# Depthwise convolution: one group's taps moved to TensorE between the key and value products

## The chip, the cores and the metric

The kernel runs on one core of a Trainium2 chip. The metric is the device time of one execution in microseconds (us). TensorE is PE in the profile's rows (PEld its weight loads), VectorE is DVE, ScalarE is ACT, GpSimd is POOL, and SyncE (SP) issues the loads.

## What is computed

Two blocks of two layers each over 512 positions of width 1024, in float32. The change lies in the second block's second layer, in its convolution module. The part of the reference that matters:

```
def conv_module(xn, w_in, b_in, dw_w, dw_b, ln_g, ln_b, w_out):
    h = xn @ w_in + b_in
    a, gate = jnp.split(h, 2, axis=-1)
    h = a * jax.nn.sigmoid(gate)
    h = lax.conv_general_dilated(
        h, dw_w[:, None, :], window_strides=(1,), padding=[(CONV_WIDTH - 1, 0)],
        dimension_numbers=('NWC', 'WIO', 'NWC'), feature_group_count=D_CONV) + dw_b
    h = jax.nn.silu(layernorm(h, ln_g, ln_b))
    return h @ w_out
...
    k = rmsnorm((memn @ wk).reshape(bsz, m_len, C_HEADS, C_HEAD_DIM), k_gain)
    v = (memn @ wv).reshape(bsz, m_len, C_HEADS, C_HEAD_DIM)
```

The convolution has 31 taps for each of 1024 channels. The keys and values are those of the cross attention that follows. They depend on the memory input alone, so they can be made while the convolution runs.

## The kernel before

**Layout.** Channels lie on the partitions in the module: eight groups g = 0 to 7 of 128 channels by 512 positions. A weight tile is loaded by SP into `raw` (three buffers) and split into two halves for a product in three passes: ACT writes the high half (L228), and DVE or GpSimd subtracts for the low half (L229, `W.low` names the engine). There are eight buffers `hl`, so a split must wait until TensorE is done with the tile eight places earlier.

**Input products.** `prod(g, j, ...)` makes the two products of a group in two PSUM banks. Then `evac(g, ...)` applies the gate: ACT reads both banks (L1439, L1440), and DVE writes `hp[:, g]` (L1441), with 30 columns of padding. No tap of a group can start before its gate.

**Taps.** A tap multiplies a shifted view of `hp` with one weight per channel. There are three ways:

- DVE: `dve_tap` (L1509, L1511) sums in a PSUM bank named by `where`.
- GpSimd: `pool_tap` sums in SBUF, in `y`. The first tap is one operation on GpSimd (L1499). For each further one ACT makes the product `m` (L1502; four buffers, so ACT's product waits for GpSimd's addition of the one four places earlier), and GpSimd adds it (L1503).
- TensorE: `diagonals` has ACT write the weights of a tap as a diagonal matrix `dg` (L1537), and `by_diagonals` multiplies it with `hp` into a bank (L1544).

`join(g)` adds DVE's or TensorE's bank to `y` (L1514, on DVE). Groups 0 to 5 had 20 taps on DVE and 11 on GpSimd. Groups 6 and 7 had 14 on TensorE, 11 on DVE and 6 on GpSimd.

**Order.** The program's order on each engine is written by a planner with a clock of its own. `steps` are TensorE's steps in order. `feed(us)` ahead of a step puts as many taps on DVE's and GpSimd's queues as fit by the costs in `T_TAP` (DVE, GpSimd). Delayed work is queued with `X.at`. Each engine then runs its instructions in that order, and waits where an operand is late.

**Keys and values.** `memory_kv` gives 16 steps of twelve matmuls: four each for two halves of the keys, then for two halves of the values. Before them the memory input is transposed on TensorE (L337, four times four blocks) and split into `xh` and `xl` (L325, L326). After each half of the keys the result is normed (ACT L999, GpSimd L321 and L322, DVE L1006), transposed (L1011) and copied (ACT L1012). Values are copied (ACT L1023).

**Layer norm.** Its statistics run over all channels. `means` sums the groups of `y` with a matrix of ones on TensorE (L1559), 16 matmuls for two halves of the positions, into banks 4 and 5. Then `norm_half(0)` and later `norm_half(1)` do for each group: subtract the mean (`spread`: DVE L1588, ACT's square L1589, temporaries `s` with three buffers), sum the squares (`total`: TensorE L1596), then once reduce (DVE L1599), take the root (GpSimd) and transpose (`across`, L1606), and scale (`scale`: DVE L1610, ACT L1611 and L1612; `apply`: DVE L1616). The output product runs on position blocks of 128; its first two need half 0. The sums of half 1 stand between its matmuls.

Before, 13 of the 16 steps of keys and values stood ahead of the layer norm, and the last three were put between the operations of `norm_half(0)` (`fill`), with GpSimd doing low halves.

## Time and profile before

| | |
|---|---|
| time, median of 3 runs | 2859.72 us (2858.93 to 2860.82) |
| the profiled execution's own time | 2861.09 us |
| its span, first to last instruction | 2859.3 us |
| TensorE, busy and mean clock granted | 96% of the span, 0.984 |
| VectorE, ScalarE, GpSimd, busy | 45%, 35%, 17% |
| window of the taps' operations on GpSimd | 2100.5 to 2235.8 us |
| window of DVE's taps and joins | 2102.2 to 2276.7 us |
| window of the layer norm's first half | 2278.0 to 2308.2 us |

All times in the document count from the span's start. A busy TensorE is not one at its peak, since the ends of matmuls are modelled. A clock of 1.0 is 2.4 GHz, and 0.5 is 1.2 GHz. The shares are means over a program whose stages have different limits.

### The profile page before, as it was taken

To read this page: it belongs to the slowest core of one execution; us is meant where nothing else is said; L and a number is where in the kernel's file an instruction comes from. 1 tells how busy PE (TensorE), PEld (TensorE's weight loads), DVE (VectorE), ACT (ScalarE), POOL (GpSimd) and SP (SyncE) were. 2 spreads that over 40 slices of the span, in tenths; PEclk is the share of its full clock that TensorE was granted. 3 is DMA by queue.
4 is the path that set the end of the run, shared out by engine and by line. 5 is a ranking of instruction groups with operands and counts; after the bars stand their busy time and mean duration, and the time that the engine had idled before them with its cause. 6 is when DMAs were issued, how large, how long until landed. Compare 5 with 4: busy or idle time off the path is not lost.

```text
span 2859.3 us, 34280 instructions
## 1 busy us (share of the span) xinstructions
PE 2744.4 (96%) x13688; PEld 2302.1 (81%) x13688; DVE 1294.8 (45%) x1952; ACT 1012.5 (35%) x1774; POOL 472.9 (17%) x483
## 2 busy tenths in 40 slices
PE   7999999999899999999999999999998789999999
PEld 7888888889788888888677888888886568888887
DVE  4565222444464323344974443223389744422232
ACT  3434222333434222334454532223266244322231
POOL 3231000013131000022450310000059223100000
PEclk9999999999999999999999999999999889999999
DMA  4222322323222333322132212333232112133231
GB/s 148 79 72 74 113 93 96 111 62 108 68 74 81 98 101 103 108 75 86 52 129 74 99 50 100 107 98 110 89 123 81 66 46 95 47 101 103 89 118 52
DMA packets 76191, 255.95 MB, mean 90 GB/s; under 512 B 10368, under 2 KB 11776, under 8 KB 76032
## 3 DMA queue, kind: packets, MB, share of 16 engines
q1 hardware_dynamic: 76032, 253.77, 27.0%
q8 instruction: 107, 1.75, 0.2%
q14 instruction: 52, 0.43, 0.0%
HBM read 251.64 MB, written 2.10 MB: 89 GB/s over the span
## 4 chain that ended last, share of the span: by engine, by line
PE 83%; DVE 7%; POOL 4%; ACT 4%; issue 2%; DMA 0%; POOLq 0%; ACTq 0%; DVEq 0%; SPq 0%
PE b L315 26%; PE b L317 25%; PE b L316 25%; POOL y L1503 2%; DVE b L1511 1%; PE b L337 1%; PE b L1395 1%; ACT hl L228 1%; DVE hl L229 1%; DVE mask L1173 1%; POOL sm L322 1%; PE b L712 1%; DVE mask L1178 0%; PE b L733 0%; PE b L747 0%
## 5 line engine op out<-in xcount | busy, mean ns | idle before, releaser
L315 PE MATMUL b<-xh,hl 128*128 128x512 f32 (+1 forms) x1728 | 641.9, 371 | 1.6 <-ACT xh L325 1.6
L316 PE MATMUL b<-xl,hl 128*128 128x512 f32 (+1 forms) x1728 | 640.8, 371 | 1.7 <-DVE xl L326 1.7
L317 PE MATMUL b<-xh,hl 128*128 128x512 f32 (+1 forms) x1728 | 640.2, 370 | 0.0
L229 DVE TENSOR_TENSOR hl<-raw,hl 128x1024 fp32r<-128x1024 f32 (+1 forms) x411 | 489.5, 1215 | 157.6 <-ACT hl L228 154.5
L228 ACT CAST hl<-raw 128x1024 fp32r<-128x1024 f32 (+1 forms) x468 | 464.5, 1016 | 102.3 <-PE b L317 65.5
L315 PE MATMUL b<-hl,xh 128*128 128x512 f32 (+2 forms) x1152 | 442.4, 384 | 3.4 <-ACT xh L1612 1.7
L317 PE MATMUL b<-hl,xl 128*128 128x512 f32 (+2 forms) x1152 | 425.8, 370 | 4.5 <-DVE xl L326 4.3
L316 PE MATMUL b<-hl,xh 128*128 128x512 f32 (+2 forms) x1152 | 425.6, 369 | 1.8 <-DVE hl L229 1.8
L315 PEld LDWEIGHTS b<-xh,hl 128*128 128x128 f32 x1728 | 326.8, 189 | 58.6 <-ACT xh L325 2.8
L316 PEld LDWEIGHTS b<-xl,hl 128*128 128x128 f32 x1728 | 326.9, 189 | 57.6 <-DVE xl L326 2.7
L317 PEld LDWEIGHTS b<-xh,hl 128*128 128x128 f32 x1728 | 326.6, 189 | 55.4
L506 DVE TENSOR_TENSOR hraw<-sg,b 128x512 f32<-128x512 f32 (+1 forms) x96 | 61.8, 643 | 675.2 <-PE b L317 658.4
L505 ACT ACTIVATE sg<-b 128x512 f32<-128x512 f32 (+1 forms) x96 | 54.0, 563 | 674.8 <-PE b L317 674.7
L315 PE MATMUL b<-hl,hh 128*128 128x512 f32 x704 | 274.5, 390 | 0.0
L317 PE MATMUL b<-hl,hlw 128*128 128x512 f32 x704 | 274.0, 389 | 0.0
L316 PE MATMUL b<-hl,hh 128*128 128x512 f32 x704 | 274.0, 389 | 0.0
L315 PEld LDWEIGHTS b<-hl,xh 128*128 128x128 f32 x1152 | 221.4, 192 | 34.0 <-issue 8.3
L317 PEld LDWEIGHTS b<-hl,xl 128*128 128x128 f32 x1152 | 220.6, 191 | 31.4 <-DVE xl L326 5.7
L316 PEld LDWEIGHTS b<-hl,xh 128*128 128x128 f32 x1152 | 221.6, 192 | 25.6 <-DVE hl L229 3.1
L326 DVE TENSOR_TENSOR hlw<-hraw,hh 128x512 fp32r<-128x512 f32 x88 | 60.5, 691 | 210.5 <-ACT hh L325 210.5
L317 PEld LDWEIGHTS b<-hl,hlw 128*128 128x128 f32 x704 | 132.2, 188 | 27.5
L316 PEld LDWEIGHTS b<-hl,hh 128*128 128x128 f32 x704 | 132.2, 188 | 27.3
(272 smaller groups left out, 2968.2 us busy)
## 6 DMA issues: line engine op xcount, KB each, us to landing
raw<-in_ws SPq DMA_DIRECT2D x400, 512.0 KB, 3.5
raw<-in_ws SPq DMA_DIRECT2D x64, 384.0 KB, 3.1
x<-in_x SPq DMA_DIRECT2D x4, 512.0 KB, 6.3
mem<-in_mem SPq DMA_DIRECT2D x4, 512.0 KB, 5.7
out<-x SPq DMA_DIRECT2D x4, 512.0 KB, 2.6
raw<-in_ws SPq DMA_DIRECT2D x4, 336.0 KB, 2.9
gain<-in_g_mix_pre SPq DMA_DIRECT2D x2, 512.0 KB, 5.5
gain<-in_g_mix_post SPq DMA_DIRECT2D x2, 512.0 KB, 5.1
```

The lines of the kernel that those rows point to most:

```text
L228: self.nc.scalar.copy(t[:, 0, :w], r[:, :w])
L229: self.low.tensor_sub(t[:, 1, :w], r[:, :w], t[:, 0, :w].bitcast(F32))
L315: PE.matmul(o, lh, rh, start=first, stop=False)
L316: PE.matmul(o, lh, rl, start=False, stop=False)
L317: PE.matmul(o, ll, rh, start=False, stop=last)
L322: G.tensor_tensor(dst, dst, nhalf[:, :n], op=OP.pow)
L326: (low or V).tensor_sub(dl, src, dh.bitcast(F32))
L337: PE.transpose(b[:, kk * P:(kk + 1) * P], xn[:, k * P:(k + 1) * P], ident)
L505: S.activation(sg[:, c0:c1], gb[:, c0:c1], AF.Silu)
L506: V.tensor_mul(hraw[:, n, c0:c1], sg[:, c0:c1], ub[:, c0:c1])
L712: PE.matmul(s[hh][:, :n], qkT["aq"][rs, pr, cols(t)], qkT["ak"][rs, pr, :n], start=True, stop=True)
L1503: G.tensor_add(y[:, g, :], y[:, g, :], m)
```

## The change

Group 6 is no longer shared with TensorE: groups 0 to 6 have 19 taps on DVE and 12 on GpSimd, and group 7 has 28 on TensorE, 3 on GpSimd and none on DVE. The 28 diagonals are made four at a time, four such tiles ahead, and TensorE multiplies them in seven pieces of four, between the transposes of the memory input and after every second step of keys and values. Group 6 now sums in bank 4, group 7 in bank 7. The planner's cost of a tap is lower on both engines. All 16 steps of keys and values stand ahead of the layer norm; from the ninth on GpSimd does the low halves, and in the layer norm DVE does again. The two transposes after the first go to banks 0 and 1.

```
-NPOOL = (11,) * 6 + (6, 6)
-NPE = 14
-KV_LN = 13
-AT_PE = 12
-T_TAP = (0.78, 1.35)
+NPOOL = (12,) * 7 + (3,)
+NPE = 28
+KV_PE = 3
+KV_OUT = 8
+T_TAP = (0.68, 1.3)
...
-                    tr = transposer(m, t, (mem["h"], mem["l"]), (6, 6) if l else (6, 7))
+                    tr = transposer(m, t, (mem["h"], mem["l"]), (6 - 5 * t, 6 * t) if l else (6, 7))
...
-        where = {g: 4 + g % 2 for g in range(KD - 2)} | {KD - 2: 7, KD - 1: 6}
+        where = {g: 4 + g % 2 for g in range(KD - 1)} | {KD - 1: 7}
...
+        def diagonals(i):
+            g = KD - 1
+            d = st["dg", i] = pl.tile([P, 4, P], F32, tag="dg", name="dg", bufs=4)
+            for j in range(4):
+                S.activation(d[:, j], ident, AF.Copy, scale=dw[:, g, 4 * i + j:4 * i + j + 1])
+
+        def by_diagonals(i):
+            g = KD - 1
+            d = st.pop(("dg", i))
+            if i == 0:
+                acc[g] = bank(where[g])
+            for j in range(4):
+                PE.matmul(acc[g], d[:, j], hp[:, g, 4 * i + j:4 * i + j + T], start=i + j == 0, stop=4 * i + j == NPE - 1)
+            if i + 4 < NPE // 4:
+                diagonals(i + 4)
+            if 4 * i + 4 == NPE:
+                begin[g] = X.now + 4.0
+                rest(g, NPE)
...
-                if not {KD - 4, KD - 3} <= joined:
+                if not {KD - 3, KD - 2} <= joined:
...
-        steps.insert(-1, (0, lambda: diagonals(KD - 2)))
+        steps.insert(-1, (0, lambda: [diagonals(i) for i in range(4)]))
...
+        for t, h in ((0, 0), (0, 1), (1, 0)):
+            beside(0.5, lambda t=t, h=h: kv["turn", t]((h,)))
+        beside(4 * 0.86, lambda: by_diagonals(0))
+        beside(0.5, lambda: kv["turn", 1]((1,)))
+        beside(4 * 0.86, lambda: by_diagonals(1))
+        for i, (us, f) in enumerate(kv_steps):
+            if i >= KV_OUT:
+                steps.append((0, lambda: setattr(W, "low", G)))
             beside(us, f)
+            if i >= KV_PE and i % 2 and 2 + (i - KV_PE) // 2 < NPE // 4:
+                beside(4 * 0.86, lambda i=i: by_diagonals(2 + (i - KV_PE) // 2))
...
-        W.low = G
-        norm_half(0, 0.45, kv_steps[KV_LN:])
+        W.low = V
+        norm_half(0, 0.45)
         X.drain()
-        W.low = V
         norm_half(1, 0.55)
```

**Where the order changes, first place.** TensorE after the last input product (its last matmul is the first row); names with numbers are PSUM banks. Before, group 6's 14 taps stand between the four transposes:

```order
L317 MATMUL b_16181<-xh,hl 128x512
L337 MATMUL b_16295<-ident,mem 128x128 x4
L1544 MATMUL b_16310<-hp,dg 128x512 x3
L337 MATMUL b_16318<-ident,mem 128x128 x4
L1544 MATMUL b_16310<-hp,dg 128x512 x4
L337 MATMUL b_16340<-ident,mem 128x128 x4
L1544 MATMUL b_16310<-hp,dg 128x512 x3
L337 MATMUL b_16361<-ident,mem 128x128 x4
L1544 MATMUL b_16310<-hp,dg 128x512 x4
L315 MATMUL b_16393<-hl,xh 128x512
```

In the changed kernel three transposes come first, and eight taps of group 7 around the fourth:

```order
L317 MATMUL b_16194<-xh,hl 128x512
L337 MATMUL b_16313<-ident,mem 128x128 x4
L337 MATMUL b_16323<-ident,mem 128x128 x4
L337 MATMUL b_16330<-ident,mem 128x128 x4
L1543 MATMUL b_16352<-hp,dg 128x512 x4
L337 MATMUL b_16362<-ident,mem 128x128 x4
L1543 MATMUL b_16352<-hp,dg 128x512 x4
L315 MATMUL b_16400<-hl,xh 128x512
```

The keys (last row) now follow 8 taps and not 14, and these are taps of group 7, whose gate is the last. The other 20 stand in fours after steps 4, 6, 8, 10 and 12 of the keys and values.

**Second place.** DVE's last taps and joins, up to the layer norm. Before (`b_16310` is group 6, `b_16737` group 7):

```order
L229 TENSOR_TENSOR hl<-raw,hl 128x1024 x3
L1511 SCALAR_TENSOR_TENSOR b_16524<-hp,conv_w,b_16524 128x512 x3
L1514 TENSOR_TENSOR y<-y,b_16524 128x512
L1511 SCALAR_TENSOR_TENSOR b_16310<-hp,conv_w,b_16310 128x512 x8
L1514 TENSOR_TENSOR y<-y,b_16310 128x512
L1511 SCALAR_TENSOR_TENSOR b_16737<-hp,conv_w,b_16737 128x512 x11
L1514 TENSOR_TENSOR y<-y,b_16737 128x512
L1588 TENSOR_TENSOR y<-y,b_16823 128x256 x8
```

In the changed kernel (`b_16641` is group 6, `b_16352` group 7):

```order
L1006 SCALAR_TENSOR_TENSOR kn<-b_16535,sm,g_15665 128x256 x2
...
L1513 TENSOR_TENSOR y<-y,b_16426 128x512
L1510 SCALAR_TENSOR_TENSOR b_16641<-hp,conv_w,b_16641 128x512 x11
L1513 TENSOR_TENSOR y<-y,b_16352 128x512
L1513 TENSOR_TENSOR y<-y,b_16641 128x512
L1589 TENSOR_TENSOR y<-y,b_16840 128x256 x8
```

Group 6 is joined last, right behind group 7. The splits are gone from this stretch. From the first gate (L1441) to the last join DVE has 30 splits before and 26 now.

**Third place.** TensorE from the last mean on. Before, the first sum of squares follows at once, and the three late steps stand between the sums (here the first of them):

```order
L1559 MATMUL b_16823<-y,ones 128x256
L1559 MATMUL b_16825<-y,ones 128x256
L1596 MATMUL b_16841<-ones,s 128x2 x2
L315 MATMUL b_16769<-hl,xh 128x512
L316 MATMUL b_16769<-hl,xh 128x512
```

In the changed kernel the thirteenth step comes ahead of the first mean, the fourteenth behind the first twelve means, and then four means and two whole steps (24 matmuls, first and last shown) ahead of the sums:

```order
L1560 MATMUL b_16840<-y,ones 128x256
L1560 MATMUL b_16842<-y,ones 128x256
L315 MATMUL b_16826<-hl,xh 128x512
...
L317 MATMUL b_16827<-hl,xl 128x512
L1597 MATMUL b_16909<-ones,s 128x2 x16
L1607 MATMUL b_16957<-ident,sm 128x128 x2
L315 MATMUL b_17009<-hl,xh 128x512
```

All eight sums now stand behind the last step. On ACT a split, which needs the fifteenth step's tile, and the copies of the last values stand among the squares:

```order
L1022 COPY vt<-b_16703 128x512
L228 CAST hl<-raw 128x1024 x3
L1590 ACTIVATE s<-y 128x256 x2
L1022 COPY vt<-b_16826 128x512
L1022 COPY vt<-b_16827 128x512
L1590 ACTIVATE s<-y 128x256 x6
L1612 ACTIVATE s<-y,conv_ln_b,conv_ln_g 128x256
L1613 CAST xh<-s 128x256
L228 CAST hl<-raw 128x1024
```

Before, the eight squares stood together there, the two copies behind them, and three splits among the scalings behind that.

## Rows read from the trace of the kernel before

**Rows 1.** The page, part 4: the chain that ended last, by engine.

```profile
PE 83%; DVE 7%; POOL 4%; ACT 4%; issue 2%; DMA 0%; POOLq 0%; ACTq 0%; DVEq 0%; SPq 0%
```

**Rows 2.** Stretches: busy us of PE, PEld, DVE, ACT, POOL; PEclk; DMA share, GB/s.

```profile
2170.00:2199.00 29.00, 18.72 (x46) 8.54 (x44) 26.05 (x34) 20.31 (x40) 26.50 (x20) 0.76 0.16 55
2199.00:2259.00 60.00, 53.49 (x202) 38.39 (x201) 52.15 (x70) 30.91 (x62) 31.95 (x27) 0.94 0.27 92
2259.00:2278.00 19.00, 7.77 (x31) 5.84 (x30) 16.92 (x23) 0.00 (x0) 0.00 (x0) 0.79 0.12 45
2278.00:2309.00 31.00, 18.61 (x78) 14.29 (x77) 12.72 (x28) 15.64 (x32) 8.45 (x6) 0.67 0.16 51
```

**Rows 3.** Timeline of DVE, 2235 to 2312: start, us, operation, count [idle before].

```profile
2240.19 8.63 DVE L1511 SCALAR_TENSOR_TENSOR b<-hp,conv_w,b 128x512 f32<-128x512 f32 x13
...
2253.95 3.48 DVE L229 TENSOR_TENSOR hl<-raw,hl 128x1024 fp32r<-128x1024 f32 x3
...
2276.01 0.69 DVE L1514 TENSOR_TENSOR y<-y,b 128x512 f32<-128x512 f32 x1
2278.01 2.74 DVE L1588 TENSOR_TENSOR y<-y,b 128x256 f32<-128x256 f32 x8 [1.31 <-PE b L1559]
2293.14 0.17 DVE L1599 TENSOR_REDUCE sm<-b 128x2 f32<-128x16 f32 x1 [12.38 <-PE b L1596]
2295.26 1.08 DVE L1610 TENSOR_TENSOR y<-y,b 128x256 f32<-128x256 f32 x3 [1.95 <-PE b L1606]
...
2308.20 2.73 DVE L1588 TENSOR_TENSOR y<-y,b 128x256 f32<-128x256 f32 x8
```

**Rows 4.** Groups by line, DVE, 2181 to 2277: busy, mean ns, idle before.

```profile
L229 DVE TENSOR_TENSOR hl<-raw,hl 128x1024 fp32r<-128x1024 f32 x13 | 19.6, 1517 | 6.6 <-ACT hl L228 6.6
```

**Rows 5.** Timeline of ACT, 2160 to 2312.

```profile
2172.85 4.20 ACT L1537 ACTIVATE dg<-ident,conv_w 128x128 f32<-128x128 f32 x14
...
2179.89 0.67 ACT L1439 ACTIVATE th<-b,hb 128x512 f32<-128x512 f32 x1
...
2182.44 1.95 ACT L1502 ACTIVATE m<-hp,conv_w 128x512 f32<-128x512 f32 x3
...
2292.17 1.05 ACT L1023 COPY vt<-b 128x512 f32<-128x512 f32 x2
...
2296.72 1.99 ACT L228 CAST hl<-raw 128x1024 fp32r<-128x1024 f32 x2
...
2308.67 1.11 ACT L1589 ACTIVATE s<-y 128x256 f32<-128x256 f32 x3
```

**Rows 6.** Timeline of POOL, 2150 to 2310 (L1499 starts groups 3, 4 and 6).

```profile
2158.75 1.73 POOL L1499 TENSOR_SCALAR y<-hp,conv_w,conv_dw_b 128x512 f32<-128x512 f32 x1
...
2176.14 1.74 POOL L1499 TENSOR_SCALAR y<-hp,conv_w,conv_dw_b 128x512 f32<-128x512 f32 x1
...
2211.55 0.77 POOL L1499 TENSOR_SCALAR y<-hp,conv_w,conv_dw_b 128x512 f32<-128x512 f32 x1
...
2234.53 1.28 POOL L1503 TENSOR_TENSOR y<-y,m 128x512 f32<-128x512 f32 x1
...
2297.84 7.36 POOL L229 TENSOR_TENSOR hl<-raw,hl 128x1024 fp32r<-128x1024 f32 x3 [3.43 <-ACT hl L228]
```

**Rows 7.** Timeline of PE between 2180 and 2350 (a tap is two records, as a mean).

```profile
2186.23 6.14 PE L1544 MATMUL b<-hp,dg 128*128 128x512 f32 x8
...
2198.69 0.79 PE L315 MATMUL b<-hl,xh 128*128 128x512 f32 x1
...
2224.89 0.60 PE L1011 MATMUL b<-ident,kn 128*128 128x128 f32 x4
2229.88 1.12 PE L1011 MATMUL b<-ident,kn 128*128 128x128 f32 x4 [4.38 <-ACT kt L1012]
...
2243.90 12.29 PE L1544 MATMUL b<-hp,dg 128*128 128x512 f32 x28 [0.68 <-ACT kt L1012]
...
2260.45 5.01 PE L1559 MATMUL b<-y,ones 128*128 128x256 f32 x22 [1.07 <-DVE y L1514]
```

More of the change, by code (lines that the diff above doesn't have):

```diff
@@ L1012, in tr @@
                     S.copy(kv["k"][:, 4 * c:4 * c + 4, cols(t)], blocks(o))
-                    mem["k"] = mem.get("k", 0) + 1
                 X.at(3.0, tr)
@@ L1048, in memory_kv @@
                 lazy(i, mk)
-        return steps, prepare, norm_mem, lambda: mem.get("k") == 4
+        return steps, prepare, norm_mem
     def sparse(pend, kv):
@@ L1260, in pooled @@
             return (24 * 0.215, go)
-        kv_steps, prepare, norm_mem, _ = memory_kv(0, pl, kv, lambda: temp()[:, :T])
+        kv_steps, prepare, norm_mem = memory_kv(0, pl, kv, lambda: temp()[:, :T])
         evacs = {"i0": idx(0), "i1": idx(1), "i2": idx(2), "q": heads("q"), "k": heads("k"), "v": heads("v")}
@@ L1523, in taps @@
             gq.extend((g, 0, 1, lambda j=j: pool_tap(g, j, j == TAPS - n)) for j in range(TAPS - n, TAPS))
-            if g < KD - 2:
+            if g < KD - 1:
                 rest(g, 0)
@@ L1529, in rest @@
             vq.append((g, 1, 1, lambda: join(g)))
-        def diagonals(g):
-            st["dg", g] = d = []
-            for i in range((NPE + 3) // 4):
-                d.append(pl.tile([P, 4, P], F32, tag="dg", name="dg", bufs=4))
-                for j in range(4 * i, min(4 * i + 4, NPE)):
-                    S.activation(d[i][:, j - 4 * i], ident, AF.Copy, scale=dw[:, g, j:j + 1])
-        def by_diagonals(g, j0, j1):
-            d = st["dg", g]
-            if j0 == 0:
-                acc[g] = bank(where[g])
-            for j in range(j0, j1):
-                PE.matmul(acc[g], d[j // 4][:, j % 4], hp[:, g, j:j + T], start=j == 0, stop=j == NPE - 1)
-            if j1 == NPE:
-                begin[g] = X.now + (j1 - j0) * 0.86 + 0.5
+        def diagonals(i):
[7 more added lines that the diff above has]
+            if i == 0:
+                acc[g] = bank(where[g])
+            for j in range(4):
[4 more added lines that the diff above has]
+                begin[g] = X.now + 4.0
                 rest(g, NPE)
@@ L1616, in apply, with norm_half @@
             V.tensor_sub(xl[:, g, h], st.pop(("w", g)), xh[:, g, h].bitcast(F32))
-        def norm_half(half, step, fill=()):
+        def norm_half(half, step):
             ops = []
@@ L1624, in norm_half @@
                     ops.append(lambda g=g: total(half, g - 1))
-            for i, (_, f) in enumerate(fill):
-                ops.insert(4 + 4 * i, f)
             ops.append(across)
@@ L1637, in norm_half @@
                 X.at(step * i, f)
-        kv_steps, prepare, norm_mem, turned_k = memory_kv(1, pl, kv, temp)
+        kv_steps, prepare, norm_mem = memory_kv(1, pl, kv, temp)
         steps = [prod(g, j, 0, 256, True, False) for g in range(2) for j in range(2)]
@@ L1644, in conv @@
         steps += [prod(g, j, 0, 512, True, True) for g in range(2, KD) for j in range(2)]
-        steps.insert(-1, (0, lambda: diagonals(KD - 2)))
+        steps.insert(-1, (0, lambda: [diagonals(i) for i in range(4)]))
         def beside(us, f):
             steps.append((us, lambda: (means(), feed(us), f())))
-        def diagonal_steps(g, between=()):
-            cut = [NPE * i // 4 for i in range(5)]
-            for i in range(4):
-                if between:
-                    beside(0.5, between[i])
-                beside(0.86 * (cut[i + 1] - cut[i]), lambda i=i: by_diagonals(g, cut[i], cut[i + 1]))
-        diagonal_steps(KD - 2, [lambda t=t, h=h: kv["turn", t]((h,)) for t in range(2) for h in range(2)])
-        for i, (us, f) in enumerate(kv_steps[:KV_LN]):
-            if i == AT_PE - 4:
-                steps.append((0, lambda: diagonals(KD - 1)))
-            if i == AT_PE:
-                steps.append((0, lambda: X.until(turned_k)))
-                diagonal_steps(KD - 1)
+        for t, h in ((0, 0), (0, 1), (1, 0)):
[6 more added lines that the diff above has]
+                steps.append((0, lambda: setattr(W, "low", G)))
             beside(us, f)
+            if i >= KV_PE and i % 2 and 2 + (i - KV_PE) // 2 < NPE // 4:
+                beside(4 * 0.86, lambda i=i: by_diagonals(2 + (i - KV_PE) // 2))
         X.at(20.0, lambda: gain("next", a["norm_cross_2"][1], "g0"))
```

## The prediction

> **What bounds the kernel now.** TensorE is 83% of the chain that ended last [rows 1], so a change pays only where TensorE is idle, and the windows over the conv module show where that is [rows 2]. From 2170.0, when the input products are done, to 2309.0, when the first half of the layer norm is done, TensorE is busy 18.72 + 53.49 + 7.77 + 18.61 = 98.6 of 139 us, and its mean clock in the four stretches is only 0.76, 0.94, 0.79 and 0.67 of full. That is 40 us of idle time, and work at half clock beside it.
>
> The DVE rows say who ends last [rows 3]. DVE runs its taps back to back to the end, and the last join begins at 2276.01. Call its end, 2276.7, T. The layer norm's first half follows: subtracting the mean starts at 2278.01 (S), the variance is reduced at 2293.14, the scaling starts at 2295.26, and the second half starts at 2308.20 (M). TensorE cannot go on with the output product in earnest before M, because the second half's sums stand between its matmuls. After M the order and the waits stay as they are, so I forecast M and carry its shift to the end.
>
> **DVE up to T.** Seven groups with 19 taps are 133, where there were 6 x 20 + 2 x 11 = 142. A tap costs 8.63/13 = 0.66 us [rows 3]: 9 x 0.66 = 5.9 us less. Of the weight splits (L229), 30 stood between the first gate and the last join, and 26 do now, since four go to GpSimd. Their mean in the stretch is 1.52 us, against 3.48/3 = 1.16 us where GpSimd is silent [rows 3, 4], so 4 x 1.52 = 6.1 us less.
>
> But DVE's order changes ahead of group 7's gate as well: 70 taps now stand before that row, not 62, and three joins, not two. Behind it are 17 fewer taps (11.2 us), four fewer splits (6.1) and one fewer join (0.6): 17.9 us less. The gate itself comes later. ACT reaches it (L1439) at 2179.89, behind the products that it makes for GpSimd's taps and behind the diagonals, 4.20 us for 14 [rows 5]. Four products can be out at once, so the last one ahead of the diagonals, now the 44th, must wait for GpSimd's 44th tap, three taps later than before; that tap ends at 2176.1, where group 4 begins [rows 6]. With a split of 1.0, 16 diagonals (4.7), three products (1.95, [rows 5]) and 0.7 for that last product, ACT is at the gate at 2184.4, 4.5 us later; with the crowding that DVE adds I take 5 us.
>
> DVE was idle some 11.5 us between 2170 and T: 2.9 + 7.9 + 2.1 in three stretches, less the 1.3 us behind T [rows 2]. If all of it stays, T = 2276.7 - 17.9 + 5 = 2263.8. If all goes, 2252.3. More than half of it, 6.6 us, was waiting for weight halves from ACT [rows 4], which was held up by 14 diagonals in one go and by TensorE's stall at 2225 to 2230 [rows 7]. The diagonals now come four at a time, but DVE waits again for keys (L1006) and splits, so I take the middle, **2258**.
>
> **Do TensorE and GpSimd allow 2258?** GpSimd ended at 2235.8, 40 us before T, and began its last 12 taps at 2211.55 [rows 6]. It gets 9 more, at (2211.55 - 2158.75)/33 = 1.60 us each, and one split ahead of group 7, 7.36/3 = 2.45 us: 2235.8 + 14.4 + 2.5 = 2252.7. That leaves 4 us. TensorE must finish group 7's 28 taps first. It resumes when the gate is through DVE, at about 2187 (before: 2186.2), spends 6.0 us on the first four taps at half clock as in the row at 2186.23, then 4 x 0.86 on the next four with a transpose, and starts the keys at about 2197 (before 2198.7) [rows 7]. A step takes (2224.89 - 2198.69 - 0.8)/9 = 2.8 us, a tap 12.29/14 = 0.88 us. Twelve steps (33.8), twenty taps (17.6), four transposes (2.4) and some 4 us of waits around the two pairs of key transposes, where before one wait alone was 4.38, give 2255. So three engines arrive within some 6 us of each other: a slip of any one is felt, which makes late likelier than early.
>
> **From T to M.** In the old order the sums for the means of groups 0 to 5 ran during DVE's last taps, since group 6 and 7 accumulated in banks 7 and 6. Now group 6 sums in bank 4, which the first mean needs, and it is joined last. So all 16 means, with a step of the values between, come after T: 12 x 0.46 (5.01/11 [rows 7]) + 2.8 + 3 x 0.46 = 9.7 us to S, where 1.3 us were. That is **8.4 us lost**, and no work hides it.
>
> Between S and the reduction 15.1 us passed, since three product steps stood between the sums of squares and ACT's squares (three buffers) waited for TensorE. Now two steps (5.6 us) stand ahead of all the sums. ACT's third split waits for the first of them and its copies of the values for the second, so six squares are left when TensorE is through: 5.6 + 1.1 + 6 x 0.37 + 0.8 for the last sum = 9.7 us, by the copies and squares in [rows 5], **5.4 us won**. The reduction to the scaling stays at 2.1 us. The scaling took 12.9 us. Three weight splits on ACT stood in it (1.99 for two [rows 5]) and one does now, but its second half goes to DVE in front of the second scaling (1.16), so ACT's waits for DVE stay: 12.9 - 2 x 1.0 = 10.9 us, **2.0 us won**. Bounds for the two gains together are 0, if ACT's waits grow by as much, and 7.4.
>
> The sum: T -18.7, to S +8.4, to the reduction -5.4, scaling -2.0: M is 17.7 us earlier. SP's loads keep their order; a split done earlier only frees its load earlier, and DMA is busy 0.12 to 0.27 [rows 2]. The profiled execution took 2861.1, 1.8 more than its span and 1.4 more than the median 2859.7, so 2843.4 there is **2842.0** as a median.
>
> **A rule that speaks against it.** When GpSimd adds, splits on DVE take 1.52 us in the mean and 1.16 alone [rows 3, 4]. The Trainium skill's "SBUF — State Buffer" (Who interferes with whom) says that DVE and GpSimd share one port pair as an exclusive lock, held for a whole instruction, against DVE operations with two SBUF inputs. The trace agrees in direction; it shows 0.36 us a split. By the rule, GpSimd's longer tap run could hold each of DVE's nine splits behind the gate for up to a full tap, 1.3 us, which would add 9 x (1.3 - 0.36) = 8.5 us to T and end at about 2850.
>
> **Rivals.** *DVE keeps its idle time* (0.24): T is 2263 to 2267, from its ordered waits or from splits that collide with GpSimd's taps as above; M is 9 to 13 us earlier, 2847 to 2851. For it: the waits are on ACT, whose queue still carries every product of GpSimd.
>
> *The gain goes into the means* (0.08): T falls by 10 only, the 8.4 us come, and squares and scaling, with their waits on ACT, save nothing near 7.4: within 5.7 us of before, 2854 to 2865. The 0.2% (5.7 us) is about what a measurement here can tell from none.
>
> *GpSimd becomes the bound, slower* (0.08). Its 87 taps, its splits and the keys' square roots stand in one queue, and ACT's in-order products wait on it, so keys' copies and splits wait too. From the 66th tap, 21 taps, a split and two pairs of roots remain; the roots took 24.3 - 12 x 1.60 = 5.1 us of the last stretch [rows 6]. At 2.4 us a tap it ends at 2211.55 + 21 x 2.4 + 5.1 + 2.5 = 2270, T 2271, and the gain is gone to 5 us; from about 2.7 us a tap the kernel is slower, and at 3.2 it is at T 2288, 2871. Against it: 33 taps ran at 1.60, contention included.
>
> *The replay holds* (0.60): T 2252 to 2262, 2836 to 2846.
>
> **How the numbers follow.** The forecast is 2842.0. The low end has DVE free of idle time (T 2252.3): 2836, set at 2834 for a scaling without the wait. The high end takes in DVE's idle time kept and part of the means' rival: 2854. Outside remain the slower case, most of the unchanged one and a little below: 0.18. Faster by over 0.2%: 0.60 + 0.24 = 0.84; within 0.08; slower 0.08.
>
> **What would show it.** DVE's last join ends at about 2258 and GpSimd's last tap at about 2253. The first mean waits for the last join and S comes 9 to 10 us after it; were the means done early, the bank argument is wrong. S to the reduction is near 10 us and scaling near 11. TensorE starts keys at about 2197 with 8 taps done. The forecast fails if GpSimd's last tap comes after 2262, if the gate comes after 2190, or if a wait of more than 3 us stands between product steps.

## The result and the profile after

The changed kernel takes 2837.79 us (median of 4 runs, 2835.86 to 2842.82), beside 2859.32 us for the kernel before in the same series (4 runs). The ratio is 0.9928, interval 0.9914 to 0.9943. The forecast was 2842.0, range 2834 to 2854. The profiled run took 2838.32 us with a span of 2836.5.

The page's chain by engine, then windows cut as in [rows 2] (busy us and number of instructions of PE, PEld, DVE, ACT, POOL; clock; DMA share, GB/s):

```profile
PE 84%; DVE 6%; POOL 4%; ACT 4%; issue 2%; DMA 0%; POOLq 0%; ACTq 0%; SPq 0%; DVEq 0%
```
```profile
2170.00:2199.00 29.00, 15.86 (x51) 9.96 (x52) 27.46 (x36) 24.12 (x51) 27.23 (x21) 0.76 0.16 55
2199.00:2259.00 60.00, 56.52 (x213) 39.51 (x212) 49.26 (x69) 32.59 (x59) 52.56 (x38) 0.97 0.34 114
2259.00:2278.00 19.00, 14.16 (x75) 11.41 (x73) 5.17 (x14) 8.21 (x16) 5.72 (x4) 0.83 0.17 56
2278.00:2309.00 31.00, 23.90 (x104) 19.67 (x105) 12.54 (x35) 13.35 (x31) 0.94 (x2) 0.78 0.05 18
```

DVE, with the rows that answer to [rows 3] (start, us, operation, count, idle time before and who ended it):

```profile
2181.97 1.02 DVE L1440 SCALAR_TENSOR_TENSOR hp<-th,av 128x512 f32<-128x512 f32 x1 [1.54 <-ACT av L1439]
...
2240.54 8.66 DVE L1510 SCALAR_TENSOR_TENSOR b<-hp,conv_w,b 128x512 f32<-128x512 f32 x11
2249.81 1.29 DVE L1513 TENSOR_TENSOR y<-y,b 128x512 f32<-128x512 f32 x2 [0.61 <-PE b L1543]
2261.74 2.74 DVE L1589 TENSOR_TENSOR y<-y,b 128x256 f32<-128x256 f32 x8 [10.65 <-PE b L1560]
2271.50 0.17 DVE L1600 TENSOR_REDUCE sm<-b 128x2 f32<-128x16 f32 x1 [7.02 <-PE b L1597]
2273.63 0.42 DVE L1611 TENSOR_TENSOR y<-y,b 128x256 f32<-128x256 f32 x1 [1.95 <-PE b L1607]
2276.16 1.23 DVE L229 TENSOR_TENSOR hl<-raw,hl 128x1024 fp32r<-128x1024 f32 x1 [2.12 <-ACT hl L228]
...
2284.89 2.73 DVE L1589 TENSOR_TENSOR y<-y,b 128x256 f32<-128x256 f32 x8
```

T is 2251.1 (2249.81 + 1.29), S 2261.74, the reduction 2271.50, the scaling 2273.63, M 2284.89. TensorE (see [rows 7]), then ACT (see [rows 5]) and GpSimd (see [rows 6]):

```profile
2183.14 5.11 PE L1543 MATMUL b<-hp,dg 128*128 128x512 f32 x8 [14.09 <-DVE hp L1440]
...
2246.11 3.60 PE L1543 MATMUL b<-hp,dg 128*128 128x512 f32 x8
...
2252.29 5.34 PE L1560 MATMUL b<-y,ones 128*128 128x256 f32 x24
...
2260.25 1.89 PE L1560 MATMUL b<-y,ones 128*128 128x256 f32 x8
```
```profile
2174.17 4.78 ACT L1535 ACTIVATE dg<-ident,conv_w 128x128 f32<-128x128 f32 x16
2178.85 1.94 ACT L1501 ACTIVATE m<-hp,conv_w 128x512 f32<-128x512 f32 x3
2180.69 0.68 ACT L1438 ACTIVATE th<-b,hb 128x512 f32<-128x512 f32 x1
```
```profile
2241.76 2.67 POOL L1502 TENSOR_TENSOR y<-y,m 128x512 f32<-128x512 f32 x2
2244.39 7.08 POOL L229 TENSOR_TENSOR hl<-raw,hl 128x1024 fp32r<-128x1024 f32 x3
```

The reader is to see three things. DVE's last joins wait for TensorE's last tap (0.61 us). TensorE's means then begin without any wait, and it is DVE that waits for them, 10.65 us. And ahead of its first tap TensorE waits 14.09 us for group 7's gate.

The start of the module differs from profile to profile though the code ahead of it is the same: its first gate (DVE's first row at 128x256 on `hp`) came at 2085.34 in the profile of before, 2080.72 in this one, and at 2077.2 to 2086.0 in the others. So all readings below count from that gate. The table has them for each kernel (us; "rest" is from M to the end of the span):

| kernel | group 7's gate | T | S | reduction | scaling | M | rest | ratio to before |
|---|---|---|---|---|---|---|---|---|
| before | 95.8 | 191.4 | 192.7 | 207.8 | 209.9 | 222.9 | 551.1 | 1 |
| changed | 101.2 | 170.4 | 181.0 | 190.8 | 192.9 | 204.2 | 551.6 | 0.9928 (0.9914 to 0.9943) |
| e1_steps_back | 101.2 | 171.2 | 179.1 | 192.4 | 194.2 | 205.4 | 551.9 | 0.9923 (0.9909 to 0.9936) |
| e2_pool11 | 101.2 | 178.7 | 190.1 | 196.4 | 198.6 | 209.8 | 550.6 | 0.9943 (0.9930 to 0.9955) |
| e4_gate_first | 99.6 | 173.3 | 184.0 | 193.7 | 195.9 | 207.1 | 552.1 | 0.9936 (0.9923 to 0.9948) |
| e5_bank | 101.2 | 173.9 | 178.9 | 188.8 | 190.9 | 202.1 | 551.0 | 0.9921 (0.9909 to 0.9934) |
| o1_norm_alone | 95.8 | 189.8 | 191.1 | 199.1 | 201.2 | 216.8 | 551.6 | 0.9981 (0.9972 to 0.9990) |
| e10_low_too | 101.2 | 170.5 | 177.5 | 190.5 | 192.4 | 202.2 | 552.1 | 0.9934 (0.9922 to 0.9946) |
| e9_npe20 | 101.2 | 174.8 | 181.7 | 189.6 | 191.7 | 204.1 | 552.7 | 0.9932 (0.9920 to 0.9944) |
| e8_behind | 101.2 | 170.4 | 171.4 | 177.6 | 179.7 | 188.2 | 556.6 | 0.9897 (0.9885 to 0.9910) |
| e11_bank_held | 101.2 | 173.0 | 180.5 | 189.8 | 192.0 | 203.2 | 552.2 | 0.9935 (0.9922 to 0.9949) |
| e3_low_dve | 101.2 | 181.1 | 188.0 | 195.1 | 197.3 | 208.5 | 551.4 | 0.9958 (0.9945 to 0.9970) |
| e6_no_add | 88.3 | 153.8 | 164.4 | 174.2 | 176.3 | 187.5 | 552.1 | one run |
| e12_gate_ahead | 92.8 | 181.9 | 183.2 | 191.3 | 193.4 | 201.9 | 550.9 | 0.9920 (0.9906 to 0.9935) |

Within the module the change is worth 222.9 - 204.2 = 18.7 us at M, of which 0.5 is given back behind it. The spans differ by 22.8; the other 4.6 us are the earlier start of the module, which the change did not make. The medians differ by 21.5 us, some 3 us more than the module's 18.2.

One profile stands behind each row of the table, and TensorE's clock alone moves such a row. Up to 153 us from the first gate the changed kernel and e1, e3, e5, e8, e10 and e11 have the same order on every engine (in e5, e8 and e11 with two banks exchanged). Yet TensorE began one and the same matmul there at 153.3 us in the changed kernel and at 154.2, 154.3, 154.0, 152.2, 152.6 and 155.9 us in these (the last section shows why). So a difference of 1 to 3 us between two rows need not come from an edit; the experiments below call this the matmul at 153 us.

Where the 18.7 us come from is seen on TensorE between group 7's gate and the reduction, in windows of before and of the changed kernel:

```profile
2181.20:2293.10 111.90, 89.93 (x334) 63.16 (x334) 87.28 (x120) 44.78 (x88) 47.73 (x39) 0.86 0.18 62
```
```profile
2182.00:2271.50 89.50, 84.64 (x332) 60.09 (x332) 69.00 (x98) 52.61 (x96) 73.13 (x52) 0.96 0.28 94
```

The work is nearly the same: 16 steps, the means and the sums, 28 taps where before had 25 (three taps of group 6 ran ahead of the gate), and one set of transposes of the memory input where before had three. But 111.9 us became 89.5: idle time fell from 22.0 to 4.9 us, and busy time from 89.93 to 84.64, at a clock of 0.96 instead of 0.86. That is 17.1 + 5.3 = 22.4 us; the gate came 5.4 later, and the scaling is 1.7 shorter. Half of the idle time of before was TensorE's waiting for DVE's joins ahead of the means (in all, times, the longest), of which the changed kernel has none:

```profile
PE b L1559 <- DVE y L1514: 11.2, 3, 8.2
```

### The profile page after: what moved, and what is told of

Read it like the earlier page. It is cut to its first block, busy times and chain, and to the rows that moved or that the text cites. A ratio compares the mean times of both kernels' runs of the same rounds, so it can differ in the third digit from the quotient of the medians.

```text
span 2836.5 us, 34303 instructions
## 1 busy us (share of the span) xinstructions
PE 2732.7 (96%) x13688; PEld 2295.1 (81%) x13688; DVE 1284.3 (45%) x1940; ACT 1020.7 (36%) x1783; POOL 494.4 (17%) x495
## 4 chain that ended last, share of the span: by engine, by line
PE 84%; DVE 6%; POOL 4%; ACT 4%; issue 2%; DMA 0%; POOLq 0%; ACTq 0%; SPq 0%; DVEq 0%
PE b L315 26%; PE b L317 26%; PE b L316 26%; POOL y L1502 2%; PE b L337 1%; PE b L1394 1%; ACT hl L228 1%; DVE mask L1172 1%; DVE hl L229 1%; POOL sm L322 1%; PE b L1543 1%; PE b L712 1%; DVE mask L1177 0%; PE b L733 0%; PE b L747 0%
## 5 line engine op out<-in xcount | busy, mean ns | idle before, releaser
L229 DVE TENSOR_TENSOR hl<-raw,hl 128x1024 fp32r<-128x1024 f32 (+1 forms) x408 | 487.3, 1219 | 154.3 <-ACT hl L228 150.8
L229 POOL TENSOR_TENSOR hl<-raw,hl 128x1024 fp32r<-128x1024 f32 (+2 forms) x60 | 142.1, 2383 | 94.0 <-ACT hl L228 93.8
```

The costliest lines, as they stand in the source:

```text
L229: self.low.tensor_sub(t[:, 1, :w], r[:, :w], t[:, 0, :w].bitcast(F32))
```

## The experiments

**The last three steps put back between the norm's operations.**

```
-        def norm_half(half, step):
+        def norm_half(half, step, fill=()):
...
+            for i, (_, f) in enumerate(fill):
+                ops.insert(4 + 4 * i, f)
             ops.append(across)
...
-        norm_half(0, 0.45)
+        norm_half(0, 0.45, kv_steps[13:])
```

> The changed kernel with one part undone: the last three steps of keys and values stand again between the operations of the layer norm's first half; the taps stay as changed. Theory (the last taps' three engines are what the change moves, the norm is a second term): the means come one step earlier, so S is 2.8 us earlier, but S to the reduction is again near 15 us instead of 9.8 and the scaling takes 2 us more: M is 4.6 us later than in the changed kernel, a ratio of about 1.0016 to it. Rival 1 (the norm free of products is the main part): 8 us or more later. Rival 2 (the steps' place is worth nothing, the short norm comes from splits moved to GpSimd): 2.8 us earlier.

M was 1.2 us later, but 0.9 of it stood at the matmul at 153 us already, ahead of the first difference in order, so 0.3 us are left for the edit. S came 1.9 earlier; S to the reduction was 13.3 us, not 15; the scaling stayed at 11.2. So it lies between my theory and rival 2: beside the new order of the taps, freeing the norm from products is worth about nothing.

**The same, with GpSimd's low halves in the norm too.**

```
-        W.low = V
-        norm_half(0, 0.45, kv_steps[13:])
+        W.low = G
+        norm_half(0, 0.45, kv_steps[13:])
         X.drain()
+        W.low = V
```

> The changed kernel with the norm's part undone wholly: the last three steps of keys and values between the operations of the norm's first half, as in the run with the steps put back, and GpSimd again for the low halves there. Theory (a split's subtraction on GpSimd, 2.4 us, holds up DVE's subtractions with two operands in SBUF, as the two of 1.42 and 2.24 us beside such splits in the trace of before suggest, where 0.42 is usual): scaling 12.5 to 13 us instead of 11.2, single DVE rows of 1.4 to 2.4 us among the 0.42 ones, and M 1.5 to 3.5 us later than with the steps alone put back. Rival (the engine of the low halves is worth nothing here, ACT's splits set the scaling): M within 0.7 us of that run.

The theory failed in its sum. DVE's subtraction beside GpSimd's split was held, as expected, past the end of the split at 2279.60:

```profile
2278.14 1.74 DVE L1617 TENSOR_TENSOR xl<-s,xh 128x256 fp32r<-128x256 f32 x1 [1.13 <-ACT xh L1613]
```
```profile
2277.25 2.35 POOL L229 TENSOR_TENSOR hl<-raw,hl 128x1024 fp32r<-128x1024 f32 x1 [5.05 <-ACT hl L228]
```

But the scaling was 9.8 us, shorter than with DVE (11.2), and M 3.2 earlier than in the run above. Of these 3.2 us 1.6 stood at the matmul at 153 us, where both runs have the same order; 1.4 lie in the scaling. On DVE the split itself stands in line ahead of the scalings and waits for ACT's high half first: 2.12 us in the row at 2276.16 of the changed kernel, and then 1.23. The runs put a price on it: with no split in it the scaling takes 8.5 us (two kernels below), with one on GpSimd 9.8, with one on DVE 11.2, with two on DVE 12.4, with three on GpSimd 12.9 (before), with four on DVE 15.6.

**The norm's part alone, in the kernel before.**

```
-KV_LN = 13
+KV_LN = 16
...
-        W.low = G
+        W.low = V
         norm_half(0, 0.45, kv_steps[KV_LN:])
```

> The kernel before with one part of the change alone: all 16 steps of keys and values ahead of the layer norm, and DVE instead of GpSimd for the low halves in its first half; taps and diagonals as before. Times count from the module's first gate. Theory (the parts overlap: TensorE is idle for 11 us before T, and three steps fit there): T and S as before (191 and 193), S to the reduction 6 to 7 us instead of 15.1, the scaling 11 to 12.9, so M 9 to 10.5 us earlier than before, a ratio to it of about 0.9965. Rival (the forecast's terms stand beside each other, 7.4 us won less one step's 2.8): M 4.6 us earlier. Rival 2 (the steps come in the way of the means and the last taps): S later by 3 us or more, M within 3 us of before.

M was 6.1 us earlier, between theory and rival. Of this 1.2 us stood at 150 us from the first gate already, where the order is still that of before, so 4.9 are left for the edit, near the rival's 4.6. S to the reduction fell by 7.2, since the steps went into TensorE's idle time ahead of T, where the last means still wait for DVE:

```profile
2260.13 6.21 PE L1559 MATMUL b<-y,ones 128*128 128x256 f32 x28
...
2269.70 2.08 PE L1559 MATMUL b<-y,ones 128*128 128x256 f32 x4 [3.37 <-DVE y L1514]
```

Four splits on DVE made the scaling 2.6 us longer, which I had not counted. Alone, the part is worth 5 to 6 us; beside the new taps it is worth -2.0 to 1.2, which is no more than single profiles differ by. Both parts use the same idle time of TensorE, so their gains don't add.

**Eleven taps of each group on GpSimd, not twelve.**

```
-NPOOL = (12,) * 7 + (3,)
+NPOOL = (11,) * 7 + (3,)
```

> The changed kernel with 11 taps of each of groups 0 to 6 on GpSimd instead of 12, so seven more on DVE. Theory (DVE's work sets T): seven times 0.66 us more on DVE, of which the 4 us of idle time that DVE has left may take 1: T 3 to 4.6 us later, and M 2 to 4.6 later, since TensorE's thirteenth step ends 1.2 us after T. Rival 1 (TensorE's chain of products and taps sets S): T moves but S by less than 1 us. Rival 2 (GpSimd or ACT's products for it set the pace): 1 us or more earlier.

T was 8.3 us later, more than the 4.6 us of work, and M 5.6, both more than expected. For the rest the rows point to a ring of waits, which no further run tested: the keys' norm came later on DVE, so TensorE's second transposes waited for ACT's copy; the steps behind them came later, and so did the splits that wait for a buffer from them, and DVE stood behind a split:

```profile
2226.75 1.11 PE L1011 MATMUL b<-ident,kn 128*128 128x128 f32 x4 [4.50 <-ACT kt L1012]
```
```profile
2233.94 1.51 DVE L229 TENSOR_TENSOR hl<-raw,hl 128x1024 fp32r<-128x1024 f32 x1 [4.15 <-ACT hl L228]
```

**Twenty taps of group 7 on TensorE, eight on DVE.**

```
-NPE = 28
+NPE = 20
```

> The changed kernel with 20 taps of group 7 on TensorE and 8 on DVE, instead of 28 and none. Theory (DVE, TensorE and GpSimd arrive together, and DVE has no room): 8 times 0.66 us on DVE behind TensorE's last tap, T 4 to 6 us later; TensorE has 7 us less to do, so it runs its steps ahead meanwhile and the way from S to the reduction gets shorter: M 2 to 5 us later. Rival 1 (TensorE is the late engine before T): T no later or earlier, M 2 us or more earlier. Rival 2 (DVE's taps make it wait for splits as with 11 taps on GpSimd): T 8 us later or more.

T was 4.4 later, as expected, but M was the same (204.1). TensorE had 7 us less to do, all 16 steps now stood ahead of the means in its order, and it waited 1.04 us for the last join:

```profile
2254.01 7.14 PE L1560 MATMUL b<-y,ones 128*128 128x256 f32 x32 [1.04 <-DVE y L1513]
```

So T can come 4.4 us later at no cost, if TensorE has that much less to do.

**The low halves of the last splits on DVE again.**

```
-            if i >= KV_OUT:
-                steps.append((0, lambda: setattr(W, "low", G)))
```

> The changed kernel with the low halves of the last splits on DVE again instead of GpSimd; DVE has seven more of them before its last join. Theory (T is DVE's, but S and the reduction are TensorE's): T 5 to 9 us later, M later by less than half of that, since TensorE goes on with its steps until the means can start. Rival (DVE sets M, as the forecast has it): M as much later as T.

T was 10.7 us later (more than expected), S 7.0, M 4.3: less than half of T's shift, as the theory has it. Here too all 16 steps came ahead of the means, and S to the reduction took 7.1 us instead of 9.8. In the changed kernel T is not what sets M; TensorE's chain is.

**The diagonals behind group 7's gate.**

```
-        steps.insert(-1, (0, lambda: [diagonals(i) for i in range(4)]))
+        steps.append((0, lambda: [diagonals(i) for i in range(4)]))
```

> The changed kernel with the 16 diagonals behind group 7's gate on ACT instead of ahead of it. TensorE stands idle for 14.1 us before its first tap, waiting for this gate. Theory (DVE's order sets the gate: it is at work until 2180.4 and then idle for 1.5 us): the gate on DVE comes 1.5 us earlier, T and M 1 to 2 us earlier. Rival 1 (ACT's diagonals set it, TensorE's 14 us are the bound): the gate and all behind it 4 us or more earlier. Rival 2 (the diagonals only move into the way of the copies of the memory input on ACT, and DVE waits for those): no gain, or up to 3 us later.

The gate came 1.7 us earlier, as DVE's order allows, but M 2.9 later: rival 2. DVE waited for ACT's copies of the memory input (1.83 and 0.40 us), and TensorE 2.26 us for the keys' norm.

**Banks exchanged, means of the first half early.**

```
-        where = {g: 4 + g % 2 for g in range(KD - 1)} | {KD - 1: 7}
+        where = {g: 5 - g % 2 for g in range(KD - 1)} | {KD - 1: 7}
...
-                if not {KD - 3, KD - 2} <= joined:
-                    break
+                if half != h or not {KD - 3, KD - 2 - (not half)} <= joined:
+                    continue
...
             ops.append(across)
+            if not half:
+                ops.append(lambda: means(True, 1))
```

> The changed kernel with the banks of even and odd groups exchanged, so that group 6 sums in bank 5 and group 5 in bank 4; the means of the first half of positions go to bank 4 as soon as group 5 is joined, and the means of the second half stand behind the transposed root of the first half. Theory (T to S is 10.6 us because the means wait for group 6's bank): of the means only four matmul records are left behind T, S comes at about 2254 instead of 2261.7, the three steps that are left then stand ahead of the sums, and the reduction is at about 2265.7 instead of 2271.5: M 5.8 us earlier, a ratio of about 0.998 to the changed kernel. Rival 1 (the sums wait for ACT's splits and TensorE's steps in any case): S is earlier, the reduction and M by less than 1.5 us. Rival 2 (the half-1 means, 3.6 us, come too late): M no earlier.

M was only 2.0 us earlier. S came 2.1 earlier, not 7, since T was 3.5 later: six means now stood ahead of group 7's last taps on TensorE, and the join waited for these.

```profile
2245.49 2.40 PE L1560 MATMUL b<-y,ones 128*128 128x256 f32 x10
...
2250.48 0.60 PE L1560 MATMUL b<-y,ones 128*128 128x256 f32 x2
...
2253.69 3.60 PE L1543 MATMUL b<-hp,dg 128*128 128x512 f32 x8
```
```profile
2257.39 1.28 DVE L1513 TENSOR_TENSOR y<-y,b 128x512 f32<-128x512 f32 x2 [3.46 <-POOL hl L229]
```

The row names GpSimd's split; TensorE's tap, which ended at 2257.29, is what came last.

**The same, with the means held until the last tap is issued.**

```
-                if half != h or not {KD - 3, KD - 2 - (not half)} <= joined:
+                if half != h or "dg_end" not in st or not {KD - 3, KD - 2 - (not half)} <= joined:
...
                 begin[g] = X.now + 4.0
+                st["dg_end"] = True
```

> The changed kernel with the banks exchanged and the first half's means held until group 7's last tap is issued, as in the run with steps behind the root, but with all 16 steps of keys and values still ahead of the sums. Only the second half's means (3.6 us of TensorE) move behind the transposed root. Theory (between group 7's gate and the reduction TensorE's own work is the bound, and the bank only sets the order within it): T as in the changed kernel, S 3 to 6 us earlier, S to the reduction longer by nearly as much, M 2.5 to 4.5 us earlier. Rival (the wait for the bank is worth its 8.4 us, as the forecast has it): M 7 us or more earlier.

M was 1.0 us earlier, less than the 2.5 to 4.5 expected. But T was 2.6 later, and this stood at the matmul at 153 us already, from TensorE's clock behind two waits (last section). Counted from that matmul, M is 3.6 us earlier, as expected. The rival's 8.4 us are not there: with the bank free, TensorE only does other work of the same length in that place.

**Three steps behind the transposed root.** As the run above, and:

```
+            for i, (_, f) in enumerate(fill[:1]):
+                ops.insert(2 + 4 * i, f)
             ops.append(across)
...
+            ops.extend(f for _, f in fill[1:])
+            ops.insert(5 if half else 0, lambda: setattr(W, "limit", W.slots if half else 0))
             for i, f in enumerate(ops):
                 X.at(step * i, f)
...
-        for i, (us, f) in enumerate(kv_steps):
+        for i, (us, f) in enumerate(kv_steps[:12]):
...
-        norm_half(0, 0.45)
+        norm_half(0, 0.45, kv_steps[12:])
```

> The changed kernel with the banks of even and odd groups exchanged, as in the earlier run, but the first means held until group 7's last tap is issued on TensorE; the thirteenth step of keys and values between the means and the sums, and the last three behind the transposed root, in TensorE's gaps beside the scaling (1.4, 1.7, 2.0 and 5.3 us in the trace of the changed kernel); the splits that wait for them come behind the scaling. Theory (M is set by what TensorE must do ahead of the reduction): T as in the changed kernel (170.4 us from the first gate), S 172.5 to 174, the reduction at about 180 instead of 190.8, M at 191 to 193 instead of 204.2; of these 11 to 13 us some 8 to 11 reach the end, since TensorE starts the output product later against M. Rival 1 (what stands behind the root is only moved past M): M earlier by as much, the end by less than 4 us. Rival 2 (ACT's splits and copies that now come behind the scaling stall the second half): no gain.

This is the fastest kernel of the study that leaves nothing out: 2827.75 us (4 runs, 2826.42 to 2832.13), and its interval lies wholly below that of the changed kernel. T is that of the changed kernel, S follows T by 1.0 us, M is 15.9 us earlier (14.8 from the matmul at 153 us), and 5.0 of these are given back behind M. In the profile 11 us reach the end; the two ratios differ by 0.0031, which is 9 us. Both lie in the 8 to 11 expected.

```profile
2249.99 3.62 PE L1561 MATMUL b<-y,ones 128*128 128x256 f32 x16
...
2256.20 3.63 PE L1598 MATMUL b<-ones,s 128*128 128x2 f32 x32
...
2261.68 6.33 PE L1561 MATMUL b<-y,ones 128*128 128x256 f32 x16
```
```profile
2253.65 2.74 DVE L1590 TENSOR_TENSOR y<-y,b 128x256 f32<-128x256 f32 x8 [1.00 <-PE b L1561]
2259.87 0.17 DVE L1601 TENSOR_REDUCE sm<-b 128x2 f32<-128x16 f32 x1 [3.48 <-PE b L1598]
```

Now DVE waits 1.00 us for the means instead of 10.65, and 3.48 for the sums instead of 7.02. Of the 15.9 us 13.2 lie ahead of the reduction and 2.7 in the scaling, in which no split stands now. It shows the bound: the taps are those of the changed kernel, and ahead of the reduction TensorE has three steps and half the means less to do. The exchange of banks by itself gave little (the two runs above).

**GpSimd's additions left out.**

```
                 S.activation(m, hp[:, g, j:j + T], AF.Copy, scale=dw[:, g, j:j + 1])
-                G.tensor_add(y[:, g, :], y[:, g, :], m)
```

> The changed kernel with GpSimd's additions of the taps left out (ACT still makes the products, DVE and TensorE do all of theirs), to see DVE and ACT without GpSimd beside them. Theory (a subtraction of two SBUF operands on DVE is held while GpSimd's addition runs, up to 1.1 us; a tap, which has one operand in SBUF, is not): every low half on DVE takes 1.2 us, where up to 2.3 us stood in groups 1 to 7, the taps stay at 0.66 us, and T is 3 to 6 us earlier; M at most 3 us earlier, since TensorE's chain stays. Rival (the long ones are waits for ACT's high half or for the buffer, put into the row): they stay at 2.1 to 2.3 us.

All 26 low halves on DVE took 1.2 us (1215 to 1442 ns), where the changed kernel has 1209 to 2318. The groups of both kernels, DVE and ACT (busy, mean ns, idle before), this one first:

```profile
L229 DVE TENSOR_TENSOR hl<-raw,hl 128x1024 fp32r<-128x1024 f32 x26 | 31.7, 1232 | 7.9 <-ACT hl L228 7.5
```
```profile
L229 DVE TENSOR_TENSOR hl<-raw,hl 128x1024 fp32r<-128x1024 f32 x25 | 40.0, 1610 | 5.1 <-ACT hl L228 4.7
```
```profile
L1501 ACT ACTIVATE m<-hp,conv_w 128x512 f32<-128x512 f32 x46 | 32.2, 723 | 23.1 <-POOL y L1502 23.1
```

The taps did not change (753 and 747 ns). T was 16.6 us earlier and M 16.7, where I had said 3 to 6 and at most 3, because the gate came 12.9 earlier, and TensorE's chain hangs on the gate. In the changed kernel ACT waits 23.1 us ahead of it for GpSimd to free buffers of products; here it waits for none, and TensorE's 14.09 us of idle time ahead of the first tap are 3.1. But DVE's rows, not ACT's waiting, make most of the 12.9 us. From the first gate to group 7's, in the changed kernel and in this one:

```profile
2080.72:2181.97 101.25, 85.73 (x452) 73.12 (x450) 91.69 (x107) 67.39 (x113) 80.88 (x57) 0.95 0.34 115
```
```profile
2080.49:2168.84 88.35, 85.19 (x452) 73.22 (x450) 79.83 (x108) 65.70 (x113) 9.82 (x12) 1.00 0.38 130
```

DVE (the third pair; 107 and 108 rows, as the gate itself lies at the window's edge) has the same rows to run and is busy 11.9 us less; its idle time fell by 1.0 only, from 9.6 to 8.5. Of the 11.9, 11.7 lie in rows with two operands in SBUF: the 17 splits took 26.8 us and take 21.1, the gates 7.9 and 5.2, the norm of the memory input 4.6 and 2.6, the product of gains 1.5 and 0.4. The taps did not get shorter.

**The gate ahead of the products.** As with three steps behind the root, and:

```
-                feed(5.2)
+                if g < KD - 1:
+                    feed(5.2)
...
-        steps.insert(-1, (0, lambda: [diagonals(i) for i in range(4)]))
+        steps.append((0, lambda: diagonals(0)))
...
             beside(0.5, lambda t=t, h=h: kv["turn", t]((h,)))
+            steps.append((0, lambda i=2 * t + h + 1: diagonals(i)))
...
-        for i, (us, f) in enumerate(kv_steps[:12]):
+        for i, (us, f) in enumerate(kv_steps[:15]):
```

> The kernel of the run with steps behind the root, with two edits: around group 7's last products no new taps are queued, and the diagonals are made in fours behind its gate, so that ACT comes to this gate without waiting for GpSimd's additions; and 15 steps of keys and values stand ahead of the means again, one between means and sums, none behind the root. Theory (TensorE's 14 us of idle time ahead of its first tap come from ACT, which stands in line behind GpSimd's additions: ACT waits 23 us for them in the changed kernel, and without additions the gate was 12.9 us earlier): the gate on DVE at 89 to 92 us from the module's first gate instead of 101.2, TensorE gains 9 to 12 us, which hold three steps; T is DVE's and stays at 167 to 171; M at 186 to 190 as in the run with steps behind the root, and the end 3 to 6 us earlier than there, since nothing is left behind the root. Rival 1 (GpSimd lacks products after the gate, and its taps, or the order of DVE, come late): T 3 us later or more, no gain over the run with steps behind the root. Rival 2 (DVE's place for the gate, not ACT, holds it): the gate at 98 us or later.

The gate came 8.4 us earlier, at 92.8, just outside the 89 to 92 expected, and TensorE's idle time ahead of its taps was 5.36 us. But rival 1 holds: T is 11.5 later and M 13.7 later than with three steps behind the root. GpSimd had no products after the gate (4.55 us of waits), and its last two taps were written behind three splits:

```profile
2255.62 2.35 POOL L229 TENSOR_TENSOR hl<-raw,hl 128x1024 fp32r<-128x1024 f32 x1 [0.81 <-ACT hl L228]
2257.92 2.61 POOL L1502 TENSOR_TENSOR y<-y,m 128x512 f32<-128x512 f32 x2
```
```profile
2260.56 0.69 DVE L1513 TENSOR_TENSOR y<-y,b 128x512 f32<-128x512 f32 x1 [7.66 <-POOL y L1502]
```

The earlier gate does not show that ACT's line behind GpSimd held it. The first edit takes eleven taps and a join from DVE's line ahead of the gate too: DVE is busy 84.7 us there instead of 91.7, which is most of the 8.4. And the gate waited for DVE, which was still at two splits, not for ACT, which was done with it at 2169.59:

```profile
2167.82 4.48 DVE L229 TENSOR_TENSOR hl<-raw,hl 128x1024 fp32r<-128x1024 f32 x2
2172.23 0.68 DVE L1440 SCALAR_TENSOR_TENSOR hp<-th,av 128x512 f32<-128x512 f32 x1
```
```profile
2168.90 0.69 ACT L1439 ACTIVATE av<-b,conv_b 128x512 f32<-128x512 f32 x1
```

With the diagonals behind the gate, too, DVE came to it without idle time. In the changed kernel DVE waited 1.54 us for ACT there, and with no additions at all its idle time ahead of the gate is 1.0 us less: that is the size of what ACT's line costs the gate. A kernel that uses the earlier gate was not found.

## Why the prediction was right, and where its reasons were not

**T.** The forecast has it 18.7 us earlier; it was 21.0 (from the span's start 2251.1, just outside my 2252 to 2262, but 4.6 us of that are the module's earlier start). DVE's idle time fell to 4.4 us of the 11.5; the middle that I took is 5.7. The gate came 5.4 us later; I had taken 5. I had worked that out from ACT's line, and DVE did wait for ACT, but 1.54 us only (0.63 before); the rest is DVE's own line, busy 91.7 us ahead of the gate instead of 84.9 with eight taps and a join more, which the forecast has as crowding. GpSimd's last tap ended 6.7 us ahead of T; I had 5.

**From T to M.** T to S was 10.6 (forecast 9.7), S to the reduction 9.76 (9.7), the root 2.13 (2.1), the scaling 11.26 (10.9). M was 18.7 us earlier; the forecast was 17.7. The lengths were read off the order of the queues, and that held. The median came 4.2 us below the forecast, and most of that is not the module's doing: the module gives 18.2 us of the 21.5, and no run explains the rest.

**The step that failed** is the reason for two of these lengths. "All 16 means come after T", so "8.4 us lost": the length is right, but the bank is not its price. With the banks exchanged M moved by 1.0 to 2.0 us only (2.7 to 3.6 from the matmul at 153 us), and half the means had left the stretch for it. And "5.4 won" and "2.0 won" in the norm are no gain of the change: undone, they are worth 1.2 us, and undone with GpSimd's low halves -2.0. I had added terms along DVE's timeline as if DVE set M. In the changed kernel TensorE does, from the gate to the reduction: 84.64 of 89.5 us busy; T moved by 4.4 us at no cost to M, when TensorE had 7 us less to do, and by 10.7 at a cost of 4.3; and three steps and half the means taken out ahead of the reduction gave 13.2 us there. In the kernel before DVE did hold TensorE up, by 11.2 us ahead of the means. The right sum is in [rows 2] already: TensorE's idle time and its half clock between the gate and the reduction, most of which the new order removed.

**The scaling.** I explained its 2.0 us by ACT's time in three splits. It was 1.7, but the size comes from the subtraction of the split: three on GpSimd held DVE's two-operand rows, one on DVE stands in its line.

**The rule against the change.** A split on DVE took 1.63 us in the mean behind the gate, nine of them, against 1.22 with the additions left out: 9 x 0.41 = 3.7 us, near the row's price (9 x 0.36 = 3.2) and not the 8.5 of the bound. The Trainium skill's "SBUF — State Buffer" (Who interferes with whom) has DVE rows with two SBUF inputs blocked by a GpSimd row that reads SBUF for as long as that lasts; the traces agree: single splits of 2.3 us, a subtraction held past 2279.6, the end of GpSimd's split, and none of the long splits once the additions are gone. It also says that DVE rows with one SBUF input, outside its two-port modes, are free of it; the taps agree, 747 and 753 ns. I had applied the rule behind the gate alone. Ahead of it the held rows cost 11.7 us, and in the kernel before presumably nearly as much (its 17 splits there took 26.5 us, against 26.8), so the change moved them little.

**The rivals.** DVE did not keep its idle time, and GpSimd's taps ran at 1.55 us in the mean, not 2.4. But GpSimd costs more than the rival saw, in another place and by another way: ahead of the gate, in DVE's rows that it holds.

## What to carry to other kernels

Where several engines meet at one point, add up each engine's own work between two fixed points; idle time and half clock of the bound engine there are the most that a new order can win, and two edits that fill the same gap don't add. Work with a later deadline belongs behind the critical join, in the gaps of the stage that follows, and here that gave some 9 us on top of the change. A slow helper can cost most where nothing is seen to wait for it: GpSimd's additions made DVE's rows 11.7 us longer ahead of the gate, while the 23.1 us for which ACT was seen to wait cost the gate some 1.5. And before a difference of a few microseconds is put down to an edit, compare the two profiles at a point ahead of the edit.

## What the runs showed of the hardware that was not expected

After the same idle time of 14.1 us the same eight records of taps took 5.11 us in the changed kernel, 5.19 to 5.94 in six others and 6.47 in one; at full clock they take 3.60. In the last, the run with the means held, the mean granted clock over these taps was 0.56, where it was 0.71 in the changed kernel; so the same order of instructions can differ by 1.4 us at each such stall:

```profile
2179.62 6.47 PE L1543 MATMUL b<-hp,dg 128*128 128x512 f32 x8 [14.11 <-DVE hp L1440]
```

The spread is wider behind TensorE's wait for ACT's copy of the first keys, which is 2.47 us in four kernels. The next 36 matmul records, the same instructions in the same order, took 9.0 us with three steps behind the root and with GpSimd's low halves in the norm, 10.6 in the changed kernel and 11.9 with the means held. The mean granted clock was 1.00 (the full 2.4 GHz) in the first two; it was 0.84 and 0.74 in the others, where some matmuls ran at 1.2 GHz. The first, third and fourth of these:

```profile
2221.00:2230.00 9.00, 9.00 (x37) 6.37 (x37) 7.32 (x10) 6.68 (x11) 8.53 (x8) 1.00 0.03 13
```
```profile
2218.90:2229.50 10.60, 10.56 (x35) 7.46 (x36) 8.86 (x10) 7.13 (x12) 10.05 (x9) 0.84 0.09 22
```
```profile
2216.70:2228.60 11.90, 11.86 (x36) 8.51 (x37) 8.16 (x10) 7.13 (x13) 11.27 (x10) 0.74 0.16 54
```

A DVE subtraction of 0.42 us took 1.42 and 2.24 us beside GpSimd's splits, in the scaling of the kernel before, while a product with one operand in PSUM took 0.41 in between:

```profile
2301.57 1.42 DVE L1616 TENSOR_TENSOR xl<-s,xh 128x256 fp32r<-128x256 f32 x1 [0.74 <-ACT xh L1612]
...
2303.24 2.24 DVE L1616 TENSOR_TENSOR xl<-s,xh 128x256 fp32r<-128x256 f32 x1
2305.41 0.41 DVE L1610 TENSOR_TENSOR y<-y,b 128x256 f32<-128x256 f32 x1
```
